# MLP weight sums prepared in DRAM, and a seven-product first MLP product in chunks 1 to 3

## The chip, the cores and the metric

The kernel runs on one core of a Trainium2 chip, in one launch. The metric is the device time of one execution in microseconds (us), the median of several runs. The core has TensorE (PE, matrix products from SBUF into PSUM), VectorE (DVE), ScalarE (ACT), GpSimd (POOL) and SyncE (SP, which here only issues transfers). Each has its own queue of instructions and works it off in order. Transfers between DRAM and SBUF go through 16 DMA engines; SP, ACT and POOL issue them.

## What is computed

One decoder layer (DEPTH is 1) on 512 tokens of width 1024, all in float32: a LayerNorm, a token mixer (gated linear attention, GLA, and multi-head latent attention, MLA, in parallel, merged by gates and projected), a second LayerNorm, a squared-ReLU MLP of hidden width 4096 and a third LayerNorm.

```python
def reference(x, positions, ...):
    cos, sin = rope_tables(positions)
    h = layer_norm(x, ln_in_g, ln_in_b)
    for l in range(DEPTH):
        mix = token_mixer(h, cos, sin, ...)
        h = layer_norm(DEEPNORM_ALPHA * h + mix, ln1_g[l], ln1_b[l])
        ff = jnp.square(jax.nn.relu(h @ w_ff1[l])) @ w_ff2[l]
        h = layer_norm(DEEPNORM_ALPHA * h + ff, ln2_g[l], ln2_b[l])
    return h
```

## The kernel before

**Products in three terms.** Every matrix operand is split into a high part (rounded to the PE's float32r format) and a low part (the rest): ACT copies the high part, DVE subtracts it (`split`, L104). A product is then three matmuls: high by high, high by low, low by high. A matmul contracts 128 rows and puts out 128 rows by up to 512 columns.

**The weight stream.** Weights come in pieces of up to 128 x 1024 numbers (512 KB). `plan` (L138) lists the pieces in `stream` in the order of use; `pump(i)` (L157), called when piece i is about to be used, issues the loads up to i + 2 on SP into a ring of three buffers (`wraw`) and the splits (L180 on ACT, L181 on DVE) into rings of two (`whi`, `wlo`) or, for some pieces, into general tiles. The order in which each engine gets its instructions is made by a scheduler that simulates the program; buffers with one tag are handed out as they come free.

**Side work.** Evictions, norms, the GLA and MLA steps are generators in the list `active`; `tick` (L208) takes a step of the first few of them after each step of a product. The GLA levels (`gla_levels`, L606) alternate between POOL (`advance`, L616: two additions), ACT (`E`, L624), DVE (`M`, L626) and PE.

**The MLP.** It runs in four chunks of 1024 hidden columns. A chunk's first product, `h1 @ w_ff1`, is a plain product: eight hidden blocks by eight blocks of depth by three terms, each matmul on all 512 tokens (`gemm_fm`, L221; results are squared in `ev_h`, L1212). The second product (`win_f2`, L1122) multiplies the 512 x 1024 hidden chunk with 1024 x 1024 of `w_ff2` as a 2 x 2 block product with seven block products in place of eight (a Winograd form). That needs sums of blocks of the hidden chunk (`win_hid`, L1104) and of the weights: T1 to T3 are made by DVE in `win_sums` (L1086), T4 in the loop (L1153), from four blocks that `win_load` (L1077) brings through POOL's queue. The seven products gather in PSUM bank pairs 0, 1, 2 and 4; each finished one is evicted by ACT (`ev`, L1163) and added to the residual `res` in SBUF by an accumulating DMA from POOL (L1165). In the last chunk the last products are added by DVE (L1182, L1189, L1192), and the closing LayerNorm of each token block (`ln2`, L1039) follows; blocks 0 to 2 are added by DMA into an output that holds the bias already (L1062, L1158).

**Pools.** General tiles of 4 KB per partition: tag A, 24 buffers. Tag C, 8 (`res` has four of them). 2 KB tiles: tag B, 22, of which the 16 tiles of `h1T`, the normalised input of the MLP, hold 16 throughout the MLP. PSUM: four banks `mm`, four `px`.

Of the kernel before, what the change touches and what calls it, by code (L numbers as in the profile page):

```python
# [19 lines left out]
P = 128  # L20
T = 512
# [31 lines left out]
def tile_hybrid_block(ctx: ExitStack, tc: tile.TileContext, I, out, dbg=None):  # L53
# [7 lines left out]
    px = ctx.enter_context(tc.tile_pool(name="px", bufs=4, space=bass.MemoryType.PSUM))  # L61

# [6 lines left out]
    TAG_C = ('h0', 'qn', 'PT1', 'res', 'bc', 'T1', 'T2')  # L69
# [64 lines left out]
    stream = []  # L134
    st = {"dma": 0, "spl": 0, "gates": ()}
# [20 lines left out]

    def pump(i):  # L157
        while st["dma"] < min(len(stream), i + 1 + DMA_AHEAD):
            e = stream[st["dma"]]
            st["dma"] += 1  # L160
            if "src" in e:
                continue
            raw = A([P, e["nk"], T * 2 // e["nk"]], F32, "wraw")
            for sl, src, cw in e["dmas"]:
                dst = raw[:, sl, :e["n"]]
                if cw is not None:
                    dst = dst.rearrange("p (h c) -> p h c", c=cw)
                nc.sync.dma_start(dst, src)
            e["raw"] = raw
        while st["spl"] < min(len(stream), i + 2 + SPLIT_AHEAD):  # L170
# [5 lines left out]
            raw = e["src"]() if "src" in e else e.pop("raw")  # L176
# [147 lines left out]
    F1 = [((0, 4), (4, 2), (6, 2))] + [tuple((b, 2) for b in range(0, 8, 2))] * 3  # L324
    HOMES = "wwrawarawawawa"
    HOME = {"w": ("whi", "wlo"), "r": ("wraw", "wraw"), "a": ("xh", "xl")}
    WIN = (("11", 0, 0), ("21", 0, 1), ("11", 1, 0), ("21", 1, 1), ("T1", 0, 2), ("T1", 1, 2), ("T2", 0, 3), ("T2", 1, 3),
           ("T4", 0, 4), ("T4", 1, 4), ("22", 0, 5), ("22", 1, 5), ("T3", 0, 6), ("T3", 1, 6))

    def win_items(ci):  # L330
        return WIN if ci < FC - 1 else WIN[:8] + WIN[10:12] + WIN[8:10] + WIN[12:]

    fb = 0
    for ci in range(FC):
        nb = 8
        for b, w in F1[ci]:
            PL["f1", ci, b] = plan("w_ff1", (fb + b) * P, w * P, res=(ci == 0 and b == 0), per=8 // w)
        PL["f2", ci] = []
        for n, (op, hf, _) in enumerate(win_items(ci)):
            PL["f2", ci].append(len(stream))  # L340
            stream.append({"src": lambda q=(ci, op, hf): WQ[q], "nk": 2, "n": T, "res": False,
                           "ahead": 2, "home": "r" if ci == FC - 1 and n == 12 else HOMES[n]})
        fb += nb
# [943 lines left out]
```

## Time and profile before

| | |
|---|---|
| median of 3 runs | 904.34 us (903.45 to 904.36) |
| profiled execution, first to last instruction (span) | 901.4 us |
| median less span | 2.94 us |
| mean granted PE clock | 0.995 |
| DMA moved | 101.47 MB, mean 113 GB/s |
| start of the MLP's first product / of the last chunk's second product | 557.8 / 850.3 us |

The profile is of one execution. Its page gives the busy time of each engine, the span in 40 slices, the chain of work that ended last and the costliest groups of instructions; other views group instructions by line and shape, list who waited for whom, and give busy time in chosen windows. Busy time of PE counts overlapping, pipelined matmuls; the pace of a row of matmuls is better read from a window's length over their number. A DMA share of 1 means that all 16 DMA engines are busy.

### The profile page before, as it was taken

The numbers are of one execution on the slowest core, as the hardware profiler recorded it, in microseconds if no ns is written. First come the engines' busy times: TensorE is split into PE (matmuls) and PEld (weight loads), VectorE is DVE, ScalarE is ACT, GpSimd is POOL, SyncE is SP. The second block draws the span as 40 slices with busy tenths as digits, with TensorE's granted clock in tenths as the row PEclk, the third lists the DMA queues.
The fourth block names the chain that finished last, engine by engine and source line by source line (L and its number), as shares of the span: only waits on it lengthen the run. The fifth ranks groups of instructions, "written<-read, shape, count | busy, mean of one in ns | idle before, by whom it ended". The sixth has DMA issues, their size and how long they took to land.

```text
span 901.4 us, 11728 instructions
## 1 busy us (share of the span) xinstructions
PE 878.1 (97%) x4472; PEld 746.5 (83%) x4472; DVE 566.1 (63%) x919; ACT 439.8 (49%) x745; POOL 172.8 (19%) x203
## 2 busy tenths in 40 slices
PE   5999999999999999999999999999999999999994
PEld 5988888888888888888888888988888888888883
DVE  7835855575635244657756797997557656754666
ACT  5555443444434333435645423366357546645654
POOL 1003442442511010000000002104400520241032
PEclk9999999999999999999999999999999999999997
DMA  7413213212213332212207618005940990397084
GB/s 243 122 47 94 90 52 94 71 47 71 75 38 93 88 105 74 68 42 65 94 24 260 205 49 303 2 0 139 302 120 25 261 249 25 80 312 169 1 210 94
DMA packets 63335, 101.47 MB, mean 113 GB/s; under 512 B 7680, under 2 KB 31616, under 8 KB 63280
## 3 DMA queue, kind: packets, MB, share of 16 engines
q1 hardware_dynamic: 48256, 64.04, 22.7%
q0 software_dynamic: 13104, 33.04, 15.2%
q10 hardware_dynamic: 1920, 3.66, 1.2%
q8 instruction: 35, 0.57, 0.3%
q14 instruction: 20, 0.16, 0.1%
HBM read 82.36 MB, written 3.67 MB: 95 GB/s over the span
## 4 chain that ended last, share of the span: by engine, by line
PE 92%; DMA 2%; ACT 2%; POOL 1%; issue 1%; DVE 1%; POOLq 0%; DVEq 0%; ACTq 0%
PE mm L231 16%; PE mm L233 15%; PE mm L232 15%; PE mm L264 6%; PE mm L265 6%; PE mm L266 6%; PE px L1141 3%; PE px L1140 3%; PE px L1142 3%; PE mm L1141 2%; PE mm L1140 2%; PE mm L1142 2%; PE px L680 2%; DMA res<-ev 1%; PE px L837 1%
## 5 line engine op out<-in xcount | busy, mean ns | idle before, releaser
L181 DVE TENSOR_TENSOR wlo<-wraw,whi 128x1024 fp32r<-128x1024 f32 (+1 forms) x104 | 117.7, 1132 | 162.3 <-ACT whi L180 154.9
L231 PE MATMUL mm<-h,whi 128*128 128x512 f32 x416 | 162.6, 392 | 0.4 <-ACT gt L924 0.4
L232 PE MATMUL mm<-h,whi 128*128 128x512 f32 x416 | 162.4, 390 | 0.0
L180 ACT ACTIVATE whi<-wraw 128x1024 fp32r<-128x1024 f32 (+1 forms) x104 | 100.3, 964 | 118.7 <-PE mm L232 68.3
L233 PE MATMUL mm<-h,wlo 128*128 128x512 f32 x416 | 154.9, 390 | 0.0
L1165 POOL DMA_DIRECT2D res<-ev x56 | 48.6, 980 | 238.2 <-ACT ev L1163 195.8
L231 PEld LDWEIGHTS mm<-h,whi 128*128 128x128 f32 x416 | 78.1, 188 | 16.3 <-ACT gt L924 0.6
L233 PEld LDWEIGHTS mm<-h,wlo 128*128 128x128 f32 x416 | 77.9, 188 | 16.4 <-DVE wlo L181 0.3
L232 PEld LDWEIGHTS mm<-h,whi 128*128 128x128 f32 x416 | 78.2, 188 | 15.6
L265 PE MATMUL mm<-wlo,h 128*128 128x512 f32 x128 | 50.3, 393 | 0.0
L266 PE MATMUL mm<-whi,h 128*128 128x512 f32 x128 | 50.1, 392 | 0.0
L264 PE MATMUL mm<-whi,h 128*128 128x512 f32 x128 | 49.7, 403 | 0.0
L1214 ACT ACTIVATE relu<-mm 128x512 f32<-128x512 f32 x32 | 18.8, 595 | 56.8 <-PE mm L233 56.8
L352 POOL TENSOR_TENSOR mv<-mv,mhalf 128x1 f32<-128x1 f32 x4 | 4.6, 1154 | 211.7 <-DVE mv L351 211.7
L619 POOL TENSOR_TENSOR rp<-rp 128x256 f32<-128x256 f32 x32 | 31.4, 983 | 60.9 <-ACT E L624 44.1
L626 DVE TENSOR_TENSOR M<-E,qk 128x512 f32<-128x512 f32 x32 | 27.3, 853 | 16.5 <-ACT E L624 16.5
L624 ACT ACTIVATE E<-rp 128x512 f32<-128x512 f32 x32 | 20.4, 638 | 26.9 <-POOL rp L620 26.9
L180 ACT ACTIVATE xh<-wraw 128x1024 fp32r<-128x1024 f32 (+1 forms) x20 | 19.0, 959 | 24.7 <-PE mm L266 16.0
L181 DVE TENSOR_TENSOR wlo<-wq,whi 128x1024 fp32r<-128x1024 f32 x15 | 18.4, 1223 | 19.7 <-ACT whi L180 19.7
L620 POOL TENSOR_TENSOR rp<-rp 128x256 f32<-128x256 f32 x32 | 27.5, 860 | 10.3 <-ACT q L649 8.1
L266 PEld LDWEIGHTS mm<-whi,h 128*128 128x128 f32 x128 | 24.0, 188 | 5.0
L265 PEld LDWEIGHTS mm<-wlo,h 128*128 128x128 f32 x128 | 24.1, 188 | 4.3
(383 smaller groups left out, 2240.9 us busy)
## 6 DMA issues: line engine op xcount, KB each, us to landing
wraw<-in_w_in_dram SPq DMA_DIRECT2D x40, 512.0 KB, 3.5
wraw<-in_w_ff_dram SPq DMA_DIRECT2D x32, 512.0 KB, 7.6
wq<-in_w_ff_dram POOLq DMA_DIRECT2D x32, 512.0 KB, 9.4
res<-ev POOLq DMA_DIRECT2D x56, 256.0 KB, 8.3
wraw<-in_w_o_gla_dram SPq DMA_DIRECT2D x8, 512.0 KB, 3.7
wraw<-in_w_o_mla_dram SPq DMA_DIRECT2D x8, 512.0 KB, 3.2
wraw<-in_w_out_dram SPq DMA_DIRECT2D x8, 512.0 KB, 4.3
wraw<-in_w_in_dram SPq DMA_DIRECT2D x8, 360.0 KB, 5.1
```

The costliest lines, as they stand in the source:

```text
L180: st["ins"] = act(hi[:, :nk, :n], raw[:, :nk, :n], AF.Copy)
L181: vtt(lo[:, :nk, :n], raw[:, :nk, :n], f(hi[:, :nk, :n]), op=ALU.subtract)
L231: mm(o, hi[:, c], xh, start=first, stop=False)
L232: mm(o, hi[:, c], xl, start=False, stop=False)
L233: mm(o, lo[:, c], xh, start=False, stop=last)
L264: mm(o, xh, hi[:, :n], start=opens, stop=False, skip_group_check=share)
L265: mm(o, xh, lo[:, :n], start=False, stop=False, skip_group_check=share)
L266: mm(o, xl, hi[:, :n], start=False, stop=last, skip_group_check=share)
L1140: mm(o, xh[:, c], hi[:, pp, cols], start=opens, stop=False, skip_group_check=True)
L1141: mm(o, xh[:, c], lo[:, pp, cols], start=False, stop=False, skip_group_check=True)
L1142: mm(o, xl[:, c], hi[:, pp, cols], start=False, stop=hf == 1 and pp == 1, skip_group_check=True)
L1165: nc.gpsimd.dma_start(res[tt + t][:, j * T:(j + 1) * T], e, accum_op=ALU.add)
```

## The change

1. **Sums in DRAM.** For seven block products (the first products of chunks 1 to 3, the second products of all four chunks), T1 to T4 are made in DRAM tiles, in two halves each: per half four copies issued on SP (t3 and t1 from block 12, t2 from t3, t4 from t2) and four accumulating DMAs issued on POOL (block 22 into t3, block 11 into t1 and into t2, block 21 into t4). `plan_side` strews these 14 x 8 = 112 transfers over the pieces from the q projection to the first four pieces of the MLP, halves interleaved, so that a transfer comes eight places after the one it needs. A copy is placed behind the last weight load on SP. `win_load`, `win_sums` and the subtraction at L1153 go.
2. **First product in seven.** In chunks 1 to 3 `win_f1` replaces `gemm_fm`: `h1` is cut into 2 x 2 blocks (512 of depth by 256 tokens), the weights likewise (512 by 512). The blocks' sums (`XS`) are made once, during the second product of chunk 0, from a float32 copy of `h1` that `ln_transpose` now writes to DRAM (`H1D`). Results are combined while they are evicted, squared by ACT and split for the second product (`relu2`, `tail`, `put`). Two of the hidden blocks are kept in the free half of `h1T`; the second of them may go there when the first block product of the second product is through (`st["p1"]`).
3. **The stream.** All pieces of the block products, sums included, are loaded by SP, up to five ahead, into a ring of the three `wraw` buffers and two of tag C (`wc`).
4. **Signs and order.** With sums that can be made by additions alone, some products enter with the opposite sign; the last product is evicted twice, with either sign. The second product's order becomes 11, 21, T4, T1, T2, 22, T3.

```diff
+    dr = ctx.enter_context(tc.tile_pool(name="dr", bufs=1, space=bass.MemoryType.DRAM))
-    TAG_C = ('h0', 'qn', 'PT1', 'res', 'bc', 'T1', 'T2')
+    TAG_C = ('h0', 'qn', 'PT1', 'res', 'bc', 'wc')
...
+    def side(i):
+        while SIDE and SIDE[0][0] <= i:
+            dst, src, add = SIDE.pop(0)[1:]
+            if add:
+                nc.gpsimd.dma_start(dst, src, accum_op=ALU.add)
+            else:
+                with tc.issue_after(st["sp"].ins):
+                    nc.sync.dma_start(dst, src)
...
+        while st["dma"] < len(stream):
             e = stream[st["dma"]]
+            if st["dma"] > i + e.get("fetch", DMA_AHEAD):
+                break
...
+            raw = A([P, e["nk"], T * 2 // e["nk"]], F32, e.get("raw", "wraw"))
...
+        side(i)
...
+    WIN = tuple((op, hf, ph) for op, ph in (("11", 0), ("21", 1), ("T4", 4), ("T1", 2), ("T2", 3), ("22", 5), ("T3", 6))
+                for hf in range(2))
+    WIN1 = tuple((op, hf, ph) for op, ph in (("11", 0), ("T1", 2), ("T2", 3), ("21", 1), ("T3", 6), ("22", 5), ("T4", 4))
+                 for hf in range(2))
...
+    def plan_win(u, items):
+        for hf in range(2):
+            t1, t2, t3, t4 = [dr.tile([P, 2, T], F32, name=nm("td")) for _ in range(4)]
+            q11, q12, q21, q22 = [quad(u, q, hf) for q in ("11", "12", "21", "22")]
...
+            parts.append(((t3, q12, 0), (t1, q12, 0)))
+            parts.append(((t3, q22, 1), (t1, q11, 1)))
+            parts.append(((t2, t3, 0),))
+            parts.append(((t2, q11, 1),))
+            parts.append(((t4, t2, 0),))
+            parts.append(((t4, q21, 1),))
...
+            raw = ("wraw", "wraw", "wraw", "wc", "wc")[st["ring"] % 5]
...
+            stream.append({"dmas": [(slice(0, 2), src, None)], "nk": 2, "n": T, "res": False, "ahead": 2,
+                           "home": home, "raw": raw, "fetch": 5})
...
+        for j, op in enumerate(ops):
+            SIDE.append((i0 + j * (i1 - i0) // len(ops),) + op)
+    plan_side(PL["q"]["idx"][0], PL["f1", 0]["idx"][-1])
...
+                if k % 4 == 3:
+                    H1D[hf, k // 4] = dr.tile([P, 4, 256], F32, name=nm("h1d"))
+                    nc.sync.dma_start(H1D[hf, k // 4], raw)
...
-    def win_load(ci):
...
-    def win_sums(ci):
...
+    def win_f1(ci, hid):
...
+        def tail():
+            for t in range(2):
+                r = R[2][:, 2 * t:2 * t + 2]
+                act(r, bank[0, t].rearrange("p (a b) -> p a b", b=256), AF.Relu)
+                act(r, r, AF.Square)
+                yield
...
+            s1 = A([P, 4, 256], F32, "hr")
+            vtt(s1, R[2], R[3], op=ALU.subtract)
+            while st["p1"] < ci:
+                yield
+            put(4, R[3])
+            yield
+            put(2, s1)
+            yield
...
+        for n, (op, hf, ph) in enumerate(WIN1):
+            pump(PL[u][n])
+            key = {3: 0, 6: 0, 4: 0, 5: 2}.get(ph, ph)
+            if (key, 0) not in bank:
+                for t in range(2):
+                    bank[key, t] = (PX if key < 2 else MM)()
...
+            for pp in range(2):
+                k = 2 * hf + pp
+                xh, xl = x(ph, k, 0), x(ph, k, 1)
+                for m in range(4):
+                    o = bank[key, m // 2][:, (m % 2) * 256:(m % 2 + 1) * 256]
+                    c = slice(m * P, (m + 1) * P)
+                    first = k == 0 and ph in (0, 1, 2) and m % 2 == 0
+                    mm(o, hi[:, pp, c], xh, start=first, stop=False, skip_group_check=True)
+                    mm(o, hi[:, pp, c], xl, start=False, stop=False, skip_group_check=True)
+                    mm(o, lo[:, pp, c], xh, start=False, stop=k == 3, skip_group_check=True)
+                tick(4)
...
+            if n == 1:
+                st["p1"] = ci
+            if ci == 0 and n == 4:
+                spawn(sums_h1())
...
+                    for tt, j, sign in (((0, 0, 1),), ((0, 0, 1),), ((2, 1, 1),), ((0, 1, -1),), ((2, 0, 1),), ((0, 1, 1),),
+                                        ((2, 0, 1), (2, 1, -1)))[ph]:
+                        e = B([P, T], F32, "ev")
+                        act(e, o, AF.Copy, scale=float(sign))
                         nc.gpsimd.dma_start(res[tt + t][:, j * T:(j + 1) * T], e, accum_op=ALU.add)
-            if n == 9 and not end:
-                win_load(ci + 1)
...
-            r2 = r.rearrange("p (j c) -> p j c", c=T)
-            vtt(r2, r2, o[:, None, :].to_broadcast([P, 2, T]), op=ALU.add)
+            vtt(r[:, T:], r[:, T:], o, op=ALU.subtract)
+            vtt(r[:, :T], r[:, :T], o, op=ALU.add)
...
+    win_f2(0, hid)
+    for ci in range(1, FC):
+        hid = [{} for _ in range(4)]
+        win_f1(ci, hid)
         win_f2(ci, hid)
```

More of the change, by code (lines that the diff above doesn't have):

```diff
@@ L323, in tile_hybrid_block @@
     FC = 4
[L324 to L328, printed above, removed]
-    def win_items(ci):
-        return WIN if ci < FC - 1 else WIN[:8] + WIN[10:12] + WIN[8:10] + WIN[12:]
@@ L333, in tile_hybrid_block @@
[L333 to L343, printed above, removed]
+    F1 = ((0, 4), (4, 2), (6, 2))
```

243 lines of the change are left out of this document (169 added, 74 removed).

## The prediction

> **What bounds the kernel now.** I read the page first, then the waits of TensorE (PE).
>
> ```profile
> span 901.4 us, 11728 instructions
> PE 878.1 (97%) x4472; PEld 746.5 (83%) x4472; DVE 566.1 (63%) x919; ACT 439.8 (49%) x745; POOL 172.8 (19%) x203
> PEclk9999999999999999999999999999999999999997
> ...
> PE px L367 <- ACT x L356: 9.1, 1, 9.1
> PE mm L233 <- DVE wlo L181: 0.5, 1, 0.5
> PE mm L231 <- ACT gt L924: 0.4, 1, 0.4
> PE mm L231 <- ACT h L370: 0.3, 1, 0.3
> ```
>
> PE waits for the first input for 9.1 us and then for 1.2 us in the whole kernel, at the full granted clock. Up to its last product the kernel is a queue of matmuls, so only a change in their number or pace moves the time, as long as their operands come in time. Next I cut the stages of the MLP out by windows (columns: stretch, length, then busy time and instruction count of each engine, granted clock, DMA share, GB/s).
>
> ```profile
> 557.70:569.20 11.50, 11.50 (x97) 11.45 (x97) 11.38 (x21) 2.13 (x3) 3.12 (x2) 1.00 0.45 158
> 605.40:643.40 38.00, 38.00 (x169) 31.47 (x168) 28.21 (x29) 22.97 (x32) 14.50 (x18) 1.00 0.68 196
> 643.60:687.00 43.40, 43.40 (x193) 35.93 (x192) 22.58 (x31) 23.14 (x35) 5.18 (x6) 1.00 0.51 119
> 725.30:768.60 43.30, 43.30 (x193) 35.87 (x192) 22.93 (x31) 23.59 (x36) 5.15 (x6) 1.00 0.50 116
> 807.00:850.20 43.20, 43.20 (x192) 35.77 (x192) 22.32 (x31) 22.54 (x34) 5.17 (x6) 1.00 0.48 111
> ```
>
> The last three are the first MLP product of chunks 1 to 3: 192 matmuls of 512 columns, 129.9 us together, 0.226 us each. The second row is the second product of chunk 0. The first row is the one place where the same kind of matmul runs on 256 columns: 96 of them (one more record lies across the edge) in 11.50 us, 0.120 us each, a little more than half of 0.226.
>
> **The matmuls.** With seven products a chunk's first product takes 7 x 4 (depth) x 4 (hidden blocks) x 3 (hi/lo terms) = 336 matmuls on 256 columns, 336 x 0.120 = 40.25 us. Three chunks take 120.8 us in place of 129.9: **-9.1 us**. The multiplications fall by an eighth (16 us), but the shorter matmul gives part of that back. The second product keeps its 168 matmuls of 512 columns.
>
> A rule stands against this price: the Trainium skill, TensorE: Matmul & The Clock Gate, section "Back-to-back issue gap", gives N/2.4 + 2.5 ns, which would make the three stages 14 us shorter. The two paces above do not bear that out (0.120 and 0.226 against its 0.109 and 0.216), so the rows are used.
>
> **Vector and scalar work, priced at nothing.** A chunk loses eight weight-sum instructions on DVE and gains six weight splits (14 pieces in place of 8), copies and adds on PSUM, and squares and splits of the hidden quadrants.
>
> ```profile
> L181 DVE TENSOR_TENSOR wlo<-wraw,whi 128x1024 fp32r<-128x1024 f32 x84 | 105.5, 1257 | 133.1 <-ACT whi L180 127.6 <-PE px L837 3.4 <-PE mm L231 1.4
> L1091 DVE TENSOR_TENSOR T<-wq,wq 128x1024 f32<-128x1024 f32 x16 | 19.3, 1219 | 0.9 <-DMA wq<-in_w_ff_dram 0.9
> L180 ACT ACTIVATE whi<-wraw 128x1024 fp32r<-128x1024 f32 x84 | 89.0, 1059 | 90.0 <-PE mm L232 47.9 <-PE mm L266 18.1 <-issue 8.6
> L1163 ACT ACTIVATE ev<-px 128x512 f32<-128x512 f32 x30 | 17.3, 596 | 17.2 <-DMA res<-ev 11.6 <-PE px L1142 2.7 <-PE mm L1142 2.6
> ```
>
> I take 1.22 us for any DVE and 1.06 us for any ACT instruction of 1024 columns, and 0.6 us for 512. First product, after: DVE 14 splits (17.1) + 6 adds of 512 (about 4) + splits of two quadrants (2.4) = 24 us; ACT 14 x 1.06 + 6 copies (3.6) + 6 relu and square (6.4) + the four of the last quadrant (2.4) + two splits (2.1) = 29 us, both under 40 us of PE. Second product: DVE 17.1 + 5 splits (6) + 4 combinations (4.9) = 28 us, ACT 14.8 + 16 evictions (9.6) + 5.3 = 30 us, under 38 us. Weights are split two pieces ahead, about 5.5 us, and this covers a late instruction of one or two microseconds. Uncovered, one late split costs its 2.3 us. At the turns between products PE could also wait for a PSUM bank: the last product of one and the first of the other both use bank pair 0. The pool has four such buffers, and those of pair 1 are emptied two or more products earlier, so the first product can open there. Nothing if that is so; else four evictions, 2.4 us, at each of six turns, 14 us.
>
> **The weights' way in the MLP.** Every piece of 512 KB (0.524 MB) now comes through SP's queue, 14 in each product, beside 16 accumulations of 256 KB per second product (14 before: the last one is evicted twice, with both signs).
>
> ```profile
> 480.00:490.00 10.00, 10.00 (x56) 8.75 (x55) 4.13 (x6) 3.62 (x6) 0.00 (x0) 1.00 1.01 369
> 875.00:880.00 5.00, 5.00 (x24) 4.14 (x23) 1.19 (x2) 0.00 (x0) 0.00 (x0) 1.00 0.79 134
> wraw<-in_w_ff_dram SPq DMA_DIRECT2D x32, 512.0 KB, 7.6
> res<-ev POOLq DMA_DIRECT2D x56, 256.0 KB, 8.3
> ACT ev L1163 <- DMA res<-ev: 37.2, 23, 5.4
> ```
>
> The first window is saturated with loads: 369 GB/s, so 1.42 us for a piece. The second holds accumulations alone: 134/0.79 = 170 GB/s, 1.55 us each. A second product then asks for 14 x 1.42 + 16 x 1.55 = 45 us of all DMA engines in 38 us, the first product for 20 us in 40; the chunk fits (65 of 78), the second product alone does not, by 7 us. With both queues served alike, weights get 19 of the 20 us they need; should accumulations go first, they are 7 us late at the end. A buffer of the five-piece ring is refilled when its split is done, and the next split of it is due five pieces, 14 us, later; less the landing time of 7.6 us, 6 us are to spare. So I price this at 0, bounds 0 and 7 us a chunk. A late accumulation holds an eviction buffer, and ACT waits for it ahead of splits; today that happens 23 times and PE doesn't feel it. Chunks 1 to 3 leave these buffers more room: the small B tiles of the old first product are gone.
>
> **The sums made ahead.** 56 copies (SP) and 56 accumulating DMAs (POOL), 512 KB each, are strewn over the 88 weight pieces from the q projection to the first block of the MLP.
>
> ```profile
> 45.00:551.00 506.00, 505.05 (x2664) 428.67 (x2664) 294.70 (x527) 225.81 (x428) 92.45 (x103) 1.00 0.28 87
> 885.00:895.00 10.00, 3.54 (x27) 3.18 (x25) 7.92 (x15) 5.83 (x12) 3.44 (x6) 0.87 0.62 100
> out_dram<-res POOLq DMA_DIRECT2D x3, 512.0 KB, 5.1
> L1062 POOL DMA_DIRECT2D out_dram<-res x3 | 2.6, 873 | 5.5 <-DVE res L1061 3.2 <-DVE mv L1065 2.3
> ```
>
> No copy from DRAM to DRAM and no accumulation from there is in the trace. The nearest rows: a load, 1.42 us, and the accumulations of `res` into the output in DRAM (the second window, 100/0.62 = 161 GB/s): 3.25 us of all engines, 0.87 us of POOL. A copy also writes DRAM, so its bounds are 1.42 and 3.25, and I take 1.7; an accumulation that reads both sides from DRAM lies between 3.25 and twice that, and I take 3.25. Sum: 56 x 1.7 + 56 x 3.25 = 277 us, on top of 0.28 x 506 = 142 us: 419 of 506 us. It fits, tightly where pieces follow fast:
>
> ```profile
> 494.00:551.00 57.00, 57.00 (x257) 47.24 (x256) 45.92 (x59) 21.03 (x25) 5.39 (x8) 1.00 0.46 148
> ...
> 494.25 18.42 SPq L168 DMA_DIRECT2D wraw<-in_w_out_dram  x8
> ...
> 512.55 0.39 PE L265 MATMUL px<-xl,mT 128*128 128x512 f32 x1
> ```
>
> Here 14 pieces bring 112/87 x 14 = 18 of the added DMAs, 45 us, to 26 us already there: 71 in 57. But the output projection's weights are issued at 494.25 and PE first uses them at 512.55, so 14 us of delay are covered by 18. I take **+1 us** here (0 to 14). The Trainium skill, DMA: Bandwidth & Descriptors, section "Latency and other measured facts", has copies between HBM tensors at 207 to 214 GB/s, 2.45 us for 512 KB; by it the sum is 461 of 506 us. No run here shows such a copy yet.
>
> On POOL the accumulations stand between the steps of the GLA levels.
>
> ```profile
> 100.00:250.00 150.00, 149.57 (x832) 129.01 (x831) 93.30 (x161) 67.82 (x130) 63.40 (x72) 1.00 0.23 69
> L624 ACT ACTIVATE E<-rp 128x512 f32<-128x512 f32 x32 | 20.4, 638 | 26.9 <-POOL rp L620 26.9
> ```
>
> A piece of 512 columns is 24 matmuls of 0.226 us, 5.4 us, so 28 pieces fall in this window; with 0.64 accumulations to a piece, 18 of them, 16 us, join 63 us of POOL work. ACT waits 26.9 us for POOL's steps, and whatever is behind `E` on ACT (weight splits, evictions) waits too; PE loses 0.43 us today. Idle POOL time takes most of it; I take **+1 us** (0 to 16, if all were on the path).
>
> **The end.** PE ends 3.5 us into the first window below, at 888.5; the rest hangs on the last accumulations:
>
> ```profile
> 885.00:890.00 5.00, 3.54 (x27) 3.18 (x25) 3.41 (x5) 4.18 (x10) 0.99 (x2) 1.00 0.64 105
> ...
> 872.52 6.16 DMA res<-ev
> ...
> 878.77 0.70 DVE res L1182
> ...
> 892.44 1.23 DVE res L1061
> ...
> L1189 DVE TENSOR_TENSOR res<-res,px x2: 1214/1215/1216, 884.2 to 886.1; 128x1024 f32<-128x1024 f32 x2
> 551.00:605.00 54.00, 53.66 (x338) 48.03 (x337) 51.14 (x86) 23.17 (x39) 5.18 (x5) 1.00 0.22 79
> ```
>
> That order stays. The pieces of items 9 to 13 now load beside these accumulations, where earlier they lay ready, and one addition (L1189, 1.22 us) becomes two of 0.70. I take **+1 us** (-1 to +4). The quadrants of h1 that are written to DRAM and read back (eight transfers of 512 KB, some 12 us) lie at the start of the MLP, where the last row leaves DMA idle for 42 of 54 us.
>
> Sum: 901.4 - 9.1 + 1 + 1 + 1 = 895.3 of span; the median is 2.94 us above this span, taken as constant: **898.2 us**, likeliest case 895 to 901.
>
> **The rivals.**
>
> (1) Weights late in the MLP. If accumulations are served first and the lead is smaller than I count, each second product costs some 2 to 3 us; four give the gain back: 898 + 8 = 906, or so near 904 as not to be told. For: 45 us of demand in 38. Against: the spare time in the first product, and landing times of 8 us that PE doesn't feel today.
>
> (2) Slower: the sums stop SP's queue. The copy t2 from t3 must wait for the accumulation eight operations earlier, on SP, ahead of all later weight loads. It decides when an accumulation takes 6.5 us rather than 3.25: then 95 + 364 + 142 = 601 us are asked of 506, POOL falls behind, copies wait, and the loads behind them with PE. Of 95 us too much the 18 us of lead and the 42 us of free DMA after 551 cover 60; the rest, 35 us, falls on PE: 898 + 35 = 933. For: the bound is real, no row shows this transfer. Against: 161 GB/s into DRAM at the end, beside other traffic.
>
> (3) POOL's issues fall on the GLA path: all 16 us there in place of 1: 913. For: the 26.9 us row. Against: POOL is busy 63 of 150 us.
>
> (4) The PSUM turns wait: 898 + 14 = 912. Against: four buffers, two of them free.
>
> **Chances.** 0.60 for the forecast, 0.12 for (1), 0.14 for (2), 0.08 for (3), 0.06 for (4). Measurements of this kernel can tell about 0.2%, 1.8 us. Faster 0.60, within 0.09 (most of (1)), slower 0.31. The range 894 to 913 leaves out (2) and the far side of the forecast.
>
> **What would show it.** PE's pace in the first product of chunks 1 to 3 at 0.120 us and 40.3 us a stage, else the first step is wrong. PE's waits by DVE `wlo` or ACT on a DMA in the MLP: rival 1; SP waiting on an accumulation and a PE wait between 480 and 600: rival 2; a PE wait of several microseconds from 100 to 250: rival 3; a PE wait for ACT evictions at the turns: rival 4. The forecast is wrong if PE's waits after the start come to more than about 5 us.

## The result and the profile after

The changed kernel takes 924.44 us (median of 4 runs, 922.28 to 927.33) beside 903.91 us of the kernel before on the same chip: ratio 1.0227, interval 1.0204 to 1.0249. It is 20 us slower; 6 us faster was forecast. The profiled execution is the slowest of the four (927.33 us). Its page:

```profile
span 925.6 us, 12963 instructions
PE 880.1 (95%) x4904; PEld 762.6 (82%) x4904; DVE 564.9 (61%) x900; ACT 470.9 (51%) x776; POOL 205.9 (22%) x227
```

PE's busy time is about what it was and the span is 24 us longer: PE waits. Its waits after the start come to 19.3 us, 1.2 before. The next table cuts each profiled execution at the first matmul of each stage (us; the columns on the right belong to experiments below).

| stage | before | after | copies only | GLA hold | split ahead | hold norm |
|---|---|---|---|---|---|---|
| up to GLA | 94.3 | 93.7 | 93.6 | 94.0 | 95.0 | 94.0 |
| GLA and the products in it | 185.7 | 192.9 | 185.8 | 185.4 | 190.5 | 187.9 |
| latent attention | 232.6 | 233.8 | 232.3 | 232.5 | 233.0 | 233.3 |
| output projection | 45.2 | 49.9 | 45.3 | 47.3 | 49.5 | 45.4 |
| first product, chunk 0 | 47.5 | 50.5 | 49.5 | 49.4 | 49.4 | 49.4 |
| second, chunk 0, and first, chunk 1 | 81.6 | 86.1 | 87.7 | 85.7 | 80.0 | 79.6 |
| second, chunk 1, to second, chunk 2 | 119.7 | 116.6 | 118.8 | 116.6 | 116.5 | 116.5 |
| first, chunk 3 | 43.5 | 43.0 | 42.9 | 44.2 | 40.3 | 40.4 |
| second, chunk 3 | 38.4 | 41.9 | 42.2 | 44.1 | 38.4 | 38.4 |
| after the last matmul | 12.9 | 17.2 | 16.7 | 16.6 | 14.5 | 15.1 |
| span | 901.4 | 925.6 | 914.8 | 915.8 | 907.1 | 900.0 |

Three first products at 40.3 us instead of 43.5 are worth 9.6 us. So the changed kernel loses 34 us elsewhere: 13 ahead of the MLP (GLA 7.2, latent attention 1.2, output projection 4.7), 3 in the first block of the MLP, 8 around the second product of chunk 0 (86.1 where 38.1 + 40.3 = 78.4 was to be had), 6 in chunk 3 and 4 at the end. Part of it is no waiting: the mean granted PE clock is 0.985, 0.995 before; a hundredth of 925 us is, by estimate, some 9 us (more on it below). Windows of the kernel before, then of the one after (length; busy time of PE, PEld, DVE, ACT, POOL; granted clock; DMA share; GB/s):

```profile
94.30:280.00 185.70, 185.27 (x1031) 159.85 (x1030) 108.34 (x192) 83.49 (x161) 71.30 (x80) 1.00 0.23 68
512.50:557.80 45.30, 45.30 (x209) 37.40 (x209) 39.33 (x57) 14.49 (x21) 7.45 (x10) 1.00 0.49 165
20.00:605.00 585.00, 583.71 (x3159) 501.57 (x3159) 367.08 (x668) 260.65 (x487) 100.22 (x109) 1.00 0.28 89
```

```profile
93.70:286.60 192.90, 188.13 (x1031) 160.62 (x1030) 106.36 (x192) 82.93 (x161) 86.63 (x96) 0.99 0.65 161
520.40:570.30 49.90, 46.43 (x210) 37.22 (x208) 40.51 (x56) 16.44 (x22) 7.53 (x7) 1.00 0.92 262
20.00:620.00 600.00, 588.51 (x3154) 502.27 (x3153) 357.79 (x661) 258.10 (x485) 149.89 (x157) 0.99 0.72 187
```

The same 1031 matmuls take 192.9 us in place of 185.7. In the last rows DMA work ahead of chunk 0's second product is 0.72 x 600 = 432 us after and 0.28 x 585 = 164 before, 268 us more. This holds the writing of `h1` too; the sums alone are set apart with e1_no_sums below.

What the waits of the changed kernel say (who waits for what: sum, times, longest):

```profile
POOL td L162 <- DMA td<-td: 172.3, 24, 28.1
POOL td L162 <- DMA td<-in_w_ff_dram: 108.4, 24, 10.2
ACT E L685 <- POOL rp L681: 38.7, 20, 5.1
ACT xh L191 <- DMA wraw<-in_w_out_dram: 17.9, 6, 4.8
```

POOL stands 281 us in front of accumulating DMAs whose copy has not landed, and whatever is behind them on POOL stands too; ACT's wait for the GLA additions has grown from 26.9 to 38.7 us. One place in GLA, on POOL, ACT and PE (start, duration, what it is; in brackets the idle time before it and what ended it):

```profile
100.86 1.05 POOL L162 DMA_DIRECT2D td<-in_w_ff_dram  x1 [4.87 <-DMA td<-in_w_ff_dram]
101.46 1.10 POOL L681 TENSOR_TENSOR rp<-rp 128x256 f32<-128x256 f32 x1
...
110.33 0.67 POOL L680 TENSOR_TENSOR rp<-rp 128x256 f32<-128x256 f32 x1 [0.74 <-ACT E L685]
113.91 1.05 POOL L162 DMA_DIRECT2D td<-in_w_ff_dram  x1 [2.91 <-DMA td<-td]
114.51 1.15 POOL L681 TENSOR_TENSOR rp<-rp 128x256 f32<-128x256 f32 x1
...
126.23 0.61 POOL L681 TENSOR_TENSOR rp<-rp 128x256 f32<-128x256 f32 x1
```

```profile
102.59 0.69 ACT L685 ACTIVATE E<-rp 128x512 f32<-128x512 f32 x1 [5.13 <-POOL rp L681]
...
115.69 0.63 ACT L685 ACTIVATE E<-rp 128x512 f32<-128x512 f32 x1 [3.52 <-POOL rp L681]
```

```profile
128.38 1.10 PE L749 MATMUL px<-M 128*128 128x256 f32 x4 [1.87 <-DVE M L687]
129.92 0.77 PE L275 MATMUL mm<-whi,h 128*128 128x512 f32 x1 [0.43 <-DVE vl L108]
130.48 0.63 PE L276 MATMUL mm<-wlo,h 128*128 128x512 f32 x1
130.91 0.63 PE L277 MATMUL mm<-whi,h 128*128 128x512 f32 x1
...
133.15 0.39 PE L277 MATMUL mm<-whi,h 128*128 128x512 f32 x1
133.38 0.40 PE L275 MATMUL mm<-whi,h 128*128 128x512 f32 x1
...
128.00:136.00 8.00, 7.18 (x25) 5.64 (x26) 7.82 (x16) 5.09 (x14) 4.86 (x6) 0.79 0.71 162
```

Twice an accumulation stands between the two additions of one level, 4.87 and 2.91 us; `E` on ACT waits 5.13 and 3.52 us for the second addition; and at the end of this chain of levels PE stands 1.87 and 0.43 us. Then PE pays again: its next matmuls start 0.43 us apart, twice the 0.23 of the last two matmuls, and the granted clock from 128 to 136 us is 0.79 (last row). So this stall of 2.3 us costs nearer 4. Not every stall does: after waits of 1.40 us at 291.8, 2.21 us at 539.9 and 1.73 us at 825.3 in the same trace the matmuls go on at full pace, with a granted clock of 1.00.

### The profile page after: what moved, and what is told of

Read it like the earlier page. It is cut to its first block, busy times and chain, and to the rows that moved or that the text cites. A ratio compares the mean times of both kernels' runs of the same rounds, so it can differ in the third digit from the quotient of the medians.

```text
span 925.6 us, 12963 instructions
## 1 busy us (share of the span) xinstructions
PE 880.1 (95%) x4904; PEld 762.6 (82%) x4904; DVE 564.9 (61%) x900; ACT 470.9 (51%) x776; POOL 205.9 (22%) x227
## 5 line engine op out<-in xcount | busy, mean ns | idle before, releaser
L162 POOL DMA_DIRECT2D td<-in_w_ff_dram x56 | 58.6, 1047 | 289.6 <-DMA td<-td 172.3
L242 PE MATMUL mm<-h,whi 128*128 128x512 f32 x224 | 87.9, 394 | 0.4 <-ACT gt L985 0.4
L243 PE MATMUL mm<-h,whi 128*128 128x512 f32 x224 | 87.6, 391 | 0.0
L244 PE MATMUL mm<-h,wlo 128*128 128x512 f32 x224 | 83.2, 391 | 1.4 <-DVE wlo L192 1.4
L192 DVE TENSOR_TENSOR xl<-wraw,xh 128x1024 fp32r<-128x1024 f32 (+1 forms) x41 | 47.3, 1159 | 47.4 <-ACT xh L191 47.4
L191 ACT ACTIVATE xh<-wraw 128x1024 fp32r<-128x1024 f32 (+1 forms) x41 | 41.2, 1008 | 61.2 <-DMA wraw<-td 17.9
L244 PEld LDWEIGHTS mm<-h,wlo 128*128 128x128 f32 x224 | 41.8, 188 | 10.4 <-DVE wlo L192 1.8
L242 PEld LDWEIGHTS mm<-h,whi 128*128 128x128 f32 x224 | 42.1, 188 | 8.9 <-ACT gt L985 0.6
L243 PEld LDWEIGHTS mm<-h,whi 128*128 128x128 f32 x224 | 42.1, 188 | 8.3
L192 DVE TENSOR_TENSOR wlo<-wc,whi 128x1024 fp32r<-128x1024 f32 x25 | 30.6, 1222 | 21.9 <-ACT whi L191 18.8
L685 ACT ACTIVATE E<-rp 128x512 f32<-128x512 f32 x32 | 20.4, 638 | 38.7 <-POOL rp L681 38.7
L191 ACT ACTIVATE whi<-wc 128x1024 fp32r<-128x1024 f32 x25 | 26.4, 1057 | 20.6 <-PE mm L1320 6.8
L1256 PE MATMUL px<-h,whi 128*128 128x256 f32 x96 | 27.8, 292 | 2.8 <-ACT whi L191 2.8
```

Of the source, the lines that this page charges most:

```text
L162: nc.gpsimd.dma_start(dst, src, accum_op=ALU.add)
L191: st["ins"] = act(hi[:, :nk, :n], raw[:, :nk, :n], AF.Copy)
L192: vtt(lo[:, :nk, :n], raw[:, :nk, :n], f(hi[:, :nk, :n]), op=ALU.subtract)
L242: mm(o, hi[:, c], xh, start=first, stop=False)
L243: mm(o, hi[:, c], xl, start=False, stop=False)
L244: mm(o, lo[:, c], xh, start=False, stop=last)
```

## The experiments

All times are medians; ratios are to runs of the kernel before made beside them (medians 903.4 to 904.1 us). Single runs of one kernel in this family spread by 1.5 to 8 us, so differences under about 3 us between two of these kernels are read from their stages, not their times.

### Which part costs what

**e1_no_sums** takes the plain blocks in place of the sums:

```diff
-            parts.append(((t3, q12, 0), (t1, q12, 0)))
...
-            TD[u, "T1", hf], TD[u, "T2", hf], TD[u, "T3", hf], TD[u, "T4", hf] = t1, t2, t3, t4
+            TD[u, "T1", hf], TD[u, "T2", hf], TD[u, "T3", hf], TD[u, "T4", hf] = q12, q11, q22, q21
```

> Leaves out: the copies and accumulating DMAs ahead of the MLP; the four combined weight pieces of each half are loaded from plain quadrants, with the same bytes in the MLP. Theory (the sums made ahead cost 7 us in GLA and 5 us in the output projection, and the rest is lost in the MLP): stages GLA 120 us and output projection 45 us as before, MLP as after; 924 less 12 to 15, 909 to 913 us. Rival (the sums run under other work for nothing, and the early losses come from something else, as the new layout of tiles): 922 to 926 us.

**e2_copies_only** drops the accumulations and keeps the copies:

```diff
-            parts.append(((t3, q22, 1), (t1, q11, 1)))
+            parts.append(())
...
```

> Leaves out: the 56 accumulating DMAs; the 56 copies stay, so that POOL's queue has nothing of the sums, and the DMA work of the accumulations is gone. Theory (GLA's loss is POOL's queue, the output projection's is the DMA engines being full): GLA 120 to 121 us, the output projection 46 to 48 us, 912 to 916 us. Rival (the SyncE queue with the copies and their bytes is what hurts): GLA still 125 us or more, 919 us or more.

**e4_no_res_add** drops the additions into `res` in chunks 0 to 2:

```diff
-                        nc.gpsimd.dma_start(res[tt + t][:, j * T:(j + 1) * T], e, accum_op=ALU.add)
+                        if end:
+                            nc.gpsimd.dma_start(res[tt + t][:, j * T:(j + 1) * T], e, accum_op=ALU.add)
```

> Leaves out: the accumulating DMAs that add the second product to the residual in chunks 0 to 2; the evictions to SBUF stay. Theory (the MLP's losses are weight pieces that arrive late because loads and accumulations fill the DMA engines): second products of chunks 0 to 2 at 38 us each and ScalarE without waits on weight loads, 924 less 6 to 10, 914 to 918 us; the last chunk's 3.6 us and the tail's 4.3 us stay. Rival (ScalarE and VectorE have too much to do with splits and sums): within 2 us of 924.

Measured: 916.82, 913.39 and 916.73 us (ratios 1.0137, 1.0112, 1.0145, intervals within 0.0023 of them). Copies alone, windows as above:

```profile
93.60:279.40 185.80, 185.37 (x1032) 159.91 (x1031) 108.38 (x192) 83.68 (x161) 71.98 (x80) 1.00 0.35 111
20.00:606.00 586.00, 583.40 (x3154) 500.69 (x3154) 360.14 (x661) 259.48 (x485) 94.91 (x101) 1.00 0.44 141
```

Everything ahead of the MLP is as before: the 13 us there belong to the accumulations, and the copies cost nothing there. Without either, the same stretch asks for 0.30 x 588 = 176 us of DMA (e1_no_sums), with the copies for 0.44 x 586 = 258, with both for 432: 1.5 us of all engines for a copy and 3.1 for an accumulation of 512 KB, and 256 us for all 112 (277 was forecast). But e1_no_sums, without any sum, is still 13 us slower than the kernel before; with the 9.6 us that should have been gained it loses 22. (909 to 913 us was expected: it loses more in the MLP than was thought.) The larger loss, then, isn't in the sums at all. Without the additions into `res` the MLP and its end take 344.1 us in place of 355.3, so DMA work in the MLP has a part in it, and the time fits the theory. But chunk 0's second product still takes 41.5 us, and PE's wait for a split in it is what it was (1.4 us at the longest, in both). So late weights are not the whole cause, as the theory had it; the runs on the MLP below show what is behind them.

### The order on POOL

**e3_pool_order** holds each accumulation behind the last POOL addition or power that the program has issued; **e6_gla_hold** only behind GLA's two additions per level:

```diff
-            gtt(Rv[:, :, 0, :], ...)
+            st["pool"] = gtt(Rv[:, :, 0, :], ...)
...
-                nc.gpsimd.dma_start(dst, src, accum_op=ALU.add)
+                with ExitStack() as gates:
+                    if "pool" in st:
+                        gates.enter_context(tc.issue_after(st["pool"].ins))
+                    nc.gpsimd.dma_start(dst, src, accum_op=ALU.add)
```

> The whole computation, with each accumulating DMA of the sums held behind the last addition of GLA that the program has on POOL so far, so that the order on POOL is the order of the program. Theory (an accumulation that waits for its copy stands ahead of GLA's additions): GLA 120 to 122 us, 917 to 920 us. Rival (the bytes of the sums, or the issue time on POOL, cost GLA its 7 us wherever they stand): GLA 126 to 128 us, 922 to 926 us.

> The whole computation, with the accumulating DMAs of the sums held behind GLA's level additions alone; once those are done, they go as in the changed kernel. Theory (GLA's 7 us are the order on POOL, the output projection's 5 us are DMA engines that are full): GLA with its neighbours 185.8 us as before, no more than 2 us lost between GLA and the output projection, the output projection still 47 to 50 us; 918 to 921 us. Rival (what is held comes as a burst afterwards and takes the 7 us back in the latent attention, as in the run with the order of the program): 923 to 926 us.

Measured: 925.62 us (1.0241, 1.0225 to 1.0256) and 918.27 us (1.016, 1.0127 to 1.0193). Both give GLA its 7 us back; e6_gla_hold:

```profile
94.00:279.40 185.40, 184.97 (x1029) 159.50 (x1027) 110.42 (x195) 82.73 (x159) 90.53 (x100) 1.00 0.68 167
```

```profile
118.62 0.95 POOL L684 TENSOR_TENSOR rp<-rp 128x256 f32<-128x256 f32 x1
```

POOL issues more here than in the changed kernel (90.5 us busy, 86.6 before) and the DMA engines are as full (0.68), so neither the issue time nor the bytes cost GLA its 7 us, only the order. ACT's wait for the additions falls from 38.7 to 28.0 us, and the addition that ended the chain of levels above at 126.23 us starts here at 118.62. e3_pool_order, expected at 917 to 920 us, lost it again later, on POOL and PE:

```profile
337.23 7.43 POOL L166 DMA_DIRECT2D td<-in_w_ff_dram  x7
```

```profile
366.25 0.58 PE L279 MATMUL mm<-whi,latT 128*128 128x256 f32 x1 [4.99 <-DVE qn L114]
```

Seven accumulations, held behind POOL's rotary additions, go out at once. PE's wait of 4.99 us follows while the DMA engines are full; that the burst causes it was not tried by itself.

### What the MLP loses

**e5_h1_local** makes the whole `h1` on POOL (16 additions of high and low halves) in place of the way through DRAM; **e7_adds_dve** lets DVE add four of a chunk's seven products (11, T4, T1 and T2) to `res` straight from PSUM; **e8_alone** has no sums, no additions by DMA in chunks 0 to 2, `h1` as in e5_h1_local and the bias writes late; **e9_bias_last** only moves the bias writes:

```diff
             q[i, j] = A([P, 4, 256], F32, "h1q")
-            nc.sync.dma_start(q[i, j], H1D[i, j])
+            for k in range(4):
...
+                gtt(q[i, j][:, k], hi, lo, op=ALU.add)
...
+                        if ph in (0, 4, 2, 3):
+                            r = res[tt + t][:, j * T:(j + 1) * T]
+                            vtt(r, r, o, op=ALU.add if sign > 0 else ALU.subtract)
+                            continue
...
-                for tt in range(3):
-                    nc.sync.dma_start(out[tt * P:(tt + 1) * P, :], gb[1])
...
+        with tc.issue_after(st["sp"].ins):
+            for tt in range(3):
+                nc.sync.dma_start(out[tt * P:(tt + 1) * P, :], gb[1])
```

> The whole computation; the normalized rows that the MLP's sums need are not written to DRAM and read back (2 MB each way), but put together on POOL from their high and low halves while POOL is idle. Theory (in the first block and the second product of chunk 0 the read-back stands ahead of weight pieces on the SyncE queue and fills the DMA engines): the second product of chunk 0 goes from 45 to 41 to 42 us, the first block of the MLP from 50.5 to 48 to 50, in all 918 to 921 us. Rival (the weight pieces and the accumulations are late there by themselves): both stages within 1 us, 923 to 926 us.

> The whole computation; half of the second product's additions to the residual (products 0, 2, 3 and 4, 8 of 16 per chunk) are made by VectorE straight from PSUM in place of an eviction on ScalarE and an accumulating DMA. Theory (in the MLP the accumulations' bytes make weight pieces late): the MLP and the tail 4 to 7 us shorter than in the changed kernel, 917 to 921 us. Rival (VectorE and ScalarE set the pace, or VectorE's splits queue behind additions that wait for PE): no gain or a loss, 923 to 930 us.

> Leaves out: the sums made ahead (plain quadrants are loaded) and the accumulating DMAs into the residual in chunks 0 to 2; the rows of the MLP's sums are put together on POOL as in the other kernel, and the three writes of the output's bias come after the last weight load. What is left is the seven-product first MLP product with its loads and vector work. Theory (the 9 us of the matmuls are real and everything lost is DMA work and its order): 893 to 898 us, with first products of 40.3 us. Rival (the new splits and sums cost PE several us by themselves): 902 to 908 us.

> The whole computation; the three writes of the output's bias on the SyncE queue are held behind the last weight load of the MLP. Theory (in the changed kernel the writes wait there for the bias row to land, and the last two weight loads stand behind them): the second product of chunk 3 from 41.8 to 38 to 40 us, the tail from 17.2 to 14 to 16 us, in all 919 to 922 us. Rival (the last pieces are late because of the splits or of full DMA engines): within 2 us of the changed kernel.

Measured: 926.51, 923.54, 911.62 and 921.18 us (ratios 1.0268, 1.0212, 1.009, 1.0202). Three of the four miss what the theory expected; the time of e9_bias_last fits, but only the end got shorter (15.6 us), while chunk 3's second product stayed at 41.7. With half the additions gone (e7_adds_dve) the time is the same, and e8_alone, with hardly any DMA work beside its weights, still loses 7 us in the second product of chunk 0 (45.5 us), where PE waits 2.4 us for a split and then runs at half pace. The changed kernel shows what stands in the way there, on ACT and on PE:

```profile
631.20 1.08 ACT L1343 ACTIVATE ev<-px 128x512 f32<-128x512 f32 x2 [0.72 <-PE px L1320]
632.17 1.06 ACT L191 ACTIVATE whi<-wc 128x1024 fp32r<-128x1024 f32 x1
```

```profile
633.28 0.73 PE L1318 MATMUL mm<-whi,a 128*128 128x512 f32 x2 [1.44 <-ACT whi L191]
```

PE has finished a product and needs the next piece; ACT first empties the finished product's two banks, for which it had to wait until that product was done, and only then splits the piece. The high half lives in a ring of two buffers, of which a piece takes the one that the piece three before it had: the split cannot start until PE is through with that one, two pieces ahead at the earliest, and evictions and a DVE split come out of these two pieces. Hence **e11_split_ahead**:

```diff
-            home = "wwa"[st["ring"] % 3] if u != ("f2", FC - 1) or n < 8 else "wawaaa"[n - 8]
+            home = "waa"[st["ring"] % 3] if u != ("f2", FC - 1) or n < 8 else "wawaaa"[n - 8]
-                           "home": home, "ahead": 2, ...
+                           "home": home, "ahead": 3, ...
...
-        while st["spl"] < min(len(stream), i + 2 + SPLIT_AHEAD):
+        while st["spl"] < min(len(stream), st["dma"]):
             e = stream[st["spl"]]
+            if st["spl"] > i + 2 and "fetch" not in e:
+                break
```

> The whole computation; weight pieces of the MLP are split three pieces ahead in place of two, and two of three pieces (in place of one) have their halves in the large ring of buffers, not in the two of whi and wlo. Theory (what is left of the losses at the starts of products, 5 to 7 us in the second product of chunk 0 and 3 us in the first product of chunk 3, is a split whose buffer or turn on ScalarE comes too late): the second product of chunk 0 from 45 to 39 to 42 us, the first product of chunk 3 to 40 to 41 us, in all 914 to 919 us. Rival (the raw pieces come too late whatever the split's lead): within 3 us of the changed kernel's 924.

Measured: 909.79 us (1.0073, 1.0058 to 1.0088), 14.6 us less than the changed kernel and better than expected. The waits around the tile `whi` from 605 to 905 us in the changed kernel (the first four rows: what its instructions waited for; after the dots: matmuls that waited for it; then, from the list of the whole run, the splits of MLP pieces that waited for their load):

```profile
  PE px L1257: 9.6, 10
  PE mm L1320: 6.8, 3
  PE mm L1257: 6.8, 4
  PE px L1320: 5.1, 3
...
  PE px L1256: 2.8, 2
  PE mm L1318: 2.1, 3
...
ACT xh L191 <- DMA wraw<-td: 17.9, 6, 4.4
ACT whi L191 <- DMA wraw<-in_w_ff_dram: 9.5, 2, 8.4
ACT xh L191 <- DMA wraw<-in_w_ff_dram: 9.4, 4, 5.8
```

and the same in e11_split_ahead, where no matmul is on the list of those that waited, followed by its windows of chunk 0's second and chunk 3's first product:

```profile
  PE px L1259: 1.8, 2
  PE mm L1259: 1.4, 1
  PE mm L1322: 0.8, 1
...
ACT whi L193 <- DMA wraw<-in_w_ff_dram: 15.7, 4, 6.7
ACT xh L193 <- DMA wraw<-td: 10.0, 5, 5.8
ACT xh L193 <- DMA wraw<-in_w_ff_dram: 7.0, 3, 3.5
```

```profile
617.40:657.50 40.10, 39.08 (x173) 31.84 (x172) 29.72 (x31) 28.05 (x39) 8.74 (x10) 1.00 0.93 265
813.90:854.20 40.30, 40.30 (x338) 40.30 (x337) 21.90 (x24) 26.34 (x36) 4.38 (x5) 1.00 0.81 244
```

The splits hardly wait for PE any more (28.3 us in these four rows, 4.0 in the three), and PE's waits for splits from chunk 0's second product on fall from 8.1 us to 0.9. The splits' waits for their loads are nearly as long as before, 32.7 us against 36.8. PE runs without a gap through a first product with the DMA engines 0.81 busy, and waits for 1 us in a second product with them 0.93 busy. So loads still come late, and PE does not feel it: what full DMA engines cost the MLP, they cost because the splits had no lead to give.

**e15_homes_only** has the buffers of e11_split_ahead with the split two ahead; **e16_no_sums_ahead** is e11_split_ahead with the plain blocks of e1_no_sums.

> The whole computation; only the place of the halves is changed (two of three pieces in the large ring), the split stays two pieces ahead. Theory (the lead of the split decides, and the two whi buffers limit it only at three pieces): 918 to 924 us. Rival (the two buffers of whi and wlo were the limit even at two pieces): 909 to 914 us.

> Leaves out: the sums made ahead (plain quadrants are loaded); splits three pieces ahead. Theory (what is lost ahead of the MLP is the sums alone, and the MLP with early splits gives the matmuls' 9 us): everything ahead of the MLP as before, first products 40.3 us and second products 38.1 us, 896 to 900 us. Rival (the MLP's loads and additions still cost it several us beside the sums): 902 us or more.

Measured: 921.22 us (1.0199, 1.0179 to 1.022), as the theory had it, and 901.61 us (0.9974, 0.9965 to 0.9984). The buffers alone bring chunk 3's first product to 40.3 us, but chunk 0's second stays at 45.3 and chunk 3's second at 41.2: the third piece of lead does the rest. A longer lead with the old buffers was not tried. Without sums the kernel is 2 us faster than the one before, not 6 as the theory had it: ahead of the MLP all is as before, chunks 2 and 3 are at their pace, and of the 9.6 us 1.9 go in the first block (49.4 us), 5 around chunk 0's second product (83.4 us for it and the next) and 1.9 at the end (14.8).

### Repairs together

**e12_best** joins e6_gla_hold, e9_bias_last and e11_split_ahead. **e10_sums_early** (e6_gla_hold with all sums ahead of the output projection), **e13_skip_out** (e6_gla_hold and e11_split_ahead, no sums from three pieces ahead of the output projection to its end) and **e14_sums_longer** (the same, spread on to the end of chunk 1's first product) ask what the output projection loses:

```diff
-            SIDE.append((i0 + j * (i1 - i0) // len(ops),) + op)
+        at = [i for i in range(i0, i1) if not PL["out"][0]["idx"][0] - 3 <= i < PL["f1", 0]["idx"][0]]
+            SIDE.append((at[j * len(at) // len(ops)],) + op)
```

> The whole computation with three repairs together: accumulating DMAs held behind GLA's additions, the bias writes behind the last weight load, splits three pieces ahead. Theory: the three gains add up, 6 for GLA, 3 to 5 for the tail, 5 to 10 for the splits: 904 to 911 us. Rival (they share one cause, so that the later two gain nothing once the first is made): 915 to 918 us.

> The whole computation with the accumulating DMAs held behind GLA's additions as before, and all sums placed between the q projection and the first piece of the output projection, none beside it. Theory (the output projection's 5 us come from the sums' DMAs beside its loads): the output projection 45 to 46 us; the latent attention holds the denser sums for 0 to 4 us; 914 to 920 us. Rival (the sums beside the output projection cost nothing that matters): the output projection still 47 us or more, and 917 us or more.

> The whole computation: accumulating DMAs held behind GLA's additions, splits three pieces ahead, and no sums issued from three weight pieces ahead of the output projection to its end. Theory (the output projection's loss of 5 us is the sums' DMAs beside its loads): output projection 45 to 47 us, the rest as in the kernel with the three repairs, 899 to 903 us. Rival (the denser sums cost as much elsewhere, as when they were all put ahead of the output projection): 905 us or more.

> As the kernel that skips the output projection, with the sums spread on to the end of chunk 1's first product, so that they are less dense. Theory (density in the latent attention costs little, and the MLP has DMA time to spare once the splits have lead): 898 to 903 us, within 2 us of the other. Rival (in the MLP the sums' DMAs and POOL's waits stand ahead of the additions to the residual and of weight loads): 904 us or more, lost in chunk 0 and 1.

Measured: 905.25 us (1.0021, 1.0011 to 1.003), 923.20 (1.0222), 909.89 (1.0078, 1.0065 to 1.0092) and 915.54 (1.0133). The first fits its theory, the other three are slower than theirs. e12_best has 19 of the 20 us back; its output projection still takes 50.7 us. With the sums kept out, the output projection takes 45.2 to 46.4 us: its loss was the sums' DMAs beside its loads. But e10_sums_early and e13_skip_out lose 9 us at the start of the latent attention, and e14_sums_longer loses 16 in chunks 0 and 1 (134.1 us from chunk 0's second product to the end of chunk 1's, 117.9 in e13_skip_out). POOL and PE of e13_skip_out:

```profile
270.00 1.05 POOL L165 DMA_DIRECT2D td<-in_w_ff_dram  x1 [11.39 <-DMA td<-td]
...
281.16 1.03 POOL L165 DMA_DIRECT2D td<-in_w_ff_dram  x1 [3.45 <-DMA td<-in_w_ff_dram]
281.73 1.52 POOL L799 TENSOR_TENSOR grs<-gss,mhalf 128x4 f32<-128x4 f32 x1
```

```profile
283.92 1.94 PE L810 MATMUL px<-ca,og 128*128 128x128 f32 x8 [5.24 <-DVE og L804]
```

It is the order on POOL once more: three accumulations wait ahead of a power of 128 x 4 numbers, GLA's output norm. **e17_hold_norm** is e13_skip_out with the accumulations held behind that too; **e18_sums_f11** also spreads the sums over chunk 1's first product (not over chunk 0's second):

```diff
-        gtt(rs, ss, mhalf[:, :NT], op=ALU.pow)
+        st["pool"] = gtt(rs, ss, mhalf[:, :NT], op=ALU.pow)
```

> The whole computation: as the kernel that skips the output projection, with the accumulating DMAs held behind GLA's power operation of the output norm as well. Theory (the order on POOL): the stage from the end of the projections to the GLA output product back from 58.4 to 50 to 52 us, 899 to 904 us in all. Rival (the DMAs are too dense there): 56 us or more in that stage, or the same us lost within the next 100 us; 907 to 911 us.

> The whole computation: as e17_hold_norm, with the sums spread over the first product of chunk 1 as well (not over the second product of chunk 0). Theory (the order on POOL decides ahead of the MLP, and there is DMA time to spare in a first product): 898 to 903 us, chunk 1 within 2 us of the kernel with the three repairs. Rival (accumulations that wait on POOL hold up the additions to the residual and their eviction buffers in the MLP): 905 us or more, lost in chunk 1.

Measured: 901.62 us (0.9979, 0.9969 to 0.9989; 9 runs, 900.86 to 902.85) and 906.75 us (1.0042, 1.0027 to 1.0057). The stage goes from 58.4 to 49.5 us. The one ahead of it goes from 184.8 to 187.9, so from GLA's start to the stage's end 6 us are gained. e17_hold_norm does the whole computation of the change and beats both kernels, the one before by 2 us (0.2%). That is also the time without any sums (e16_no_sums_ahead, 901.61), but not by the same stages: e17_hold_norm loses 2.2 us in GLA, e16_no_sums_ahead 3.8 more around chunk 0's second product.

```profile
span 900.0 us, 12961 instructions
PE 870.4 (97%) x4904; PEld 758.8 (84%) x4904; DVE 566.8 (63%) x900; ACT 469.1 (52%) x776; POOL 207.1 (23%) x227
```

```profile
POOL td L165 <- DMA td<-td: 173.9, 18, 50.8
```

POOL waits for copies from one DRAM tile to another as long as in the changed kernel, 174 us (for all copies 230 in place of 281); now little that PE needs stands behind these waits, and PE's waits after the start come to 5.6 us in the whole run. e18_sums_f11 misses its 898 to 903 us and loses 8 us in chunk 1: in this MLP there was no room for sums.

## Why the prediction was wrong

- **The matmuls** were right: 0.120 us each was used for 40.25 us a stage, and 40.3 is what chunk 3 takes once nothing is late (e11_split_ahead, 338 matmuls). In the changed kernel as it stands only chunk 2 has the gain whole; chunk 1's first product starts with waits of 1.1 and 0.7 us and some 2 us at half pace (41.3 us).
- **Vector and scalar work, priced at nothing: the first of two steps that failed, 14 us.** It counted busy time, and rightly (30 of 38 us forecast for ACT, 28 measured in e11_split_ahead), and gave the splits "two pieces ahead, about 5.5 us". Two pieces were the most there could be, not what was left after the evictions that ACT must take first and the DVE split that follows. The warning that it gave itself, 2.3 us for an uncovered split, came true at the start of products: 8 us around chunk 0's second product and 6 us in chunk 3, half-pace matmuls included. The lead of three pieces, with buffers for it, took 12.4 of these 14 us away without any change in the work.
- **The weights' way in the MLP, 0 with bounds 0 and 7 us a chunk**: the demand was counted about rightly (65 us a chunk; 0.93 x 40.1 + 0.81 x 40.3 = 70 measured), and rival 1 named the symptom, but not its cause. Loads did come late, and in e4_no_res_add, without the accumulations, 11 us were back; but with a longer lead the DMA engines at 0.8 to 0.9 of their time cost PE next to nothing. The lead was counted for the load alone; load and split draw on the same lead.
- **The sums made ahead, +1 and +1: the second step that failed, 13 us.** The DMA work was sized well: 1.5 and 3.1 us for a copy and an accumulation (1.7 and 3.25 forecast; the 2.45 us a copy that the prediction cites beside its own price did not show), 256 us in all (277). On POOL the step counted 16 us of issuing and left out the waiting: an accumulation that waits for its copy holds all of POOL, so 281 us of waits were put into its queue, 7.2 us of which reached PE in GLA. "Eight places after the one it needs" is an order of the program; POOL's queue had the accumulations earlier. What stands behind a waiting instruction was asked of SP (rival 2) and not of POOL. Rival 3 had the place of GLA's loss, but not its size (16 us), and another mechanism. In the output projection 14 us of delay were set against 18 us of lead; 4.7 came through, and went when the sums did (e13_skip_out, e14_sums_longer).
- **Rival 2** had the sign and, by luck, nearly the time, 933 us, but not the mechanism: SP waited 0.8 us for accumulations, and an accumulation took 3.1 us, not 6.5. **Rival 4** did not show: no wait of PE for an eviction is in the trace of the changed kernel (e15_homes_only has one, 3.7 us).
- **The end, +1 with bounds -1 and +4: measured 4.3.** e9_bias_last tried the bias writes ahead of the last two loads: 1.6 us of it at most. e11_split_ahead has 2.7 less than the changed kernel; the rest stays open.
- **Not priced at all**: the first block of the MLP, 3 us longer, and about 2 in every kernel here that has the new first product, with sums or without. PE's transposes wait there for DVE's float32 copy of `h1`, 1.8 us in the changed kernel and 1.3 in e17_hold_norm, none before. e5_h1_local, which writes nothing to DRAM but puts POOL work there, has the same wait (1.5 us) and took 53.1 us; so the writing alone does not explain it, and the cause stays open.

## What to carry to other kernels

Count lead from the last thing that must happen before a buffer can be filled to the first use, less everything that is ahead in line on each engine on the way; a share of busy time says nothing of it, and one more piece of lead can be worth more than the work saved. Before a DMA that waits for another is put on a compute engine's queue, list what that engine still owes to the critical path: a small operation of a microsecond behind it can cost whatever the DMA waits. Work made ahead is not free where its transfers and a stage's own loads together fill the DMA engines (the output projection: a DMA share of 0.49 before, 0.92 with the sums beside it).

## What was not expected of the hardware

After some waits of 1.4 to 2.4 us PE ran at half pace for 3 to 4 us: 0.43 us a matmul in place of 0.23 after 1.87 and 0.43 us of waiting (above), and likewise after 1.44 us at 633.3. After others of the same length it did not: at the same place in the output projection 2.21 us of waiting left the pace whole in the changed kernel, and 2.43 us halved it in e11_split_ahead. The Trainium skill, TensorE: Matmul & The Clock Gate, section "What's actually happening", gives an idle window of about 3.4 us ahead of the half clock, with free-running bounds; here a wait of half that length was enough at times. An accumulation of 512 KB from DRAM into DRAM takes twice the DMA time of a copy (3.1 and 1.5 us) and 1.05 us of POOL to issue.
